# Attention with the scores of two key tiles side by side, then two value calls, two maxima tiles and two portions of filler

## The chip, the cores and the metric

The kernel runs on one core of one Trainium2 chip. The metric is device time in microseconds (us), the median of several executions; less is better. PE is TensorE (matrix multiplication), PEld its weight loads, DVE is VectorE, ACT is ScalarE, POOL is GpSimd, SP issues the DMAs. SBUF is the on-chip memory, PSUM the memory that matmuls write to.

## The reference

The whole program is one forward pass of two layers over 512 latent tokens and 256 context tokens of width 1024, all in float32: attention, a gated feed-forward network, a bidirectional Mamba-2 mixer, another feed-forward network. The change touches the attention alone, of which this is the core:

```
def gqa_attend(q, k, v):
    s = jnp.einsum('bqhgd,bkhd->bhgqk', q, k).astype(jnp.float32) * (HEAD_DIM ** -0.5)
    p = jax.nn.softmax(s, axis=-1).astype(v.dtype)
    return jnp.einsum('bhgqk,bkhd->bqhgd', p, v)
...
    # latent queries: all 512 latent and 256 context keys; context queries: the 256 context keys only
    k_all = jnp.concatenate([k_l, k_c], axis=1)
    v_all = jnp.concatenate([v_l, v_c], axis=1)
    ...
    o_c = gqa_attend(q_c, k_c, v_c).reshape(bsz, l_ctx, Q_DIM) @ w_o
```

There are 16 query heads of 64 dimensions and 4 key/value heads.

## The kernel before

Query heads are worked on in eight pairs, p = 0 to 7; a pair shares its key/value head, and its two heads lie in the two halves of the 128 partitions (`S64`). Float32 operands are split into a high and a low part (`qh`, `ql`, `kh`, `kl`), so each product is a sum of three matmuls.

`Pair.steps` runs over seven score tiles. Tiles 0 to 5 hold 128 keys each (512 latent, 256 context) against the 512 latent queries; tile 6 holds the 256 context queries against both context key tiles. For each tile PE computes the scores with keys on the partitions, in `ps_s`: three products (line 796) and a product of ones with a diagonal that subtracts each query's maximum (line 798). These matmuls contract over 64 rows, and the two heads use the two halves of the array at once (shape 64*128). ACT takes the exponential into `pr` (line 799); DVE adds the tiles into `acc` (lines 804 and 806, 810 for tile 6).

A step hands back a function for later, which the loop over pairs calls one step later: the values (`values`, line 760), probabilities times V in `ps_o`, with 64 output columns for each head side by side (shape 128*64). At tile 5 `final` follows: the sums (`ps_sum`, line 766), their reciprocal by a logarithm and an exponential on ACT (769, 770), and three DVE instructions (771 to 773: o, u, o). Tile 6 has its own values and sums in `ps_oc`, and its result goes to DRAM for pairs 0 to 5.

`Pair.maxima` is a generator with seven parts; in each, PE computes scores of the next pair with queries on the partitions (`ps_m`, line 724, shape 64*128) and DVE reduces them (line 726). The seventh part ends with the minima `mz` (742) and the diagonal `diag` (747), which the next pair's line 798 reads.

The filler is other matmuls that keep PE busy: the queries' projections of later pairs (`ps_q`), the adaptive modulation (`ps_ada`, `ps_adt`), norms (`ssq`), and the output projection of finished pairs (`ps_d`), with the ACT and DVE work that belongs to them. `Weave.step` issues about an equal share of it at each of the 56 steps, and runs "lights" (`normed` chains, weight splits) and loads that come due at numbered steps. Line numbers of the filler are 105, 106 and 108 (`mm3`), 128, 134 and 640.

The buffers that matter: `ps_s` and `ps_m` share tag S with two buffers of two PSUM banks; `ps_o`, `ps_sum`, `ps_oc` and all filler share four PSUM banks, tag B; `pr` has three buffers, `acc` one.

In this part of the program the order of each engine's instructions is set at build time by the framework's planner: it goes through program order, and takes on each engine the earliest instruction that it expects to be ready and to have its buffer. The chip then runs each engine's list in order. In the first stage of the attention (up to the query, key and value projections) the order is that of the program.

Of the kernel before, what the change touches and what calls it, by code (L numbers as in the profile page):

```python
# [7 lines left out]
P = 128  # L8
F32 = mybir.dt.float32
F32R = mybir.dt.float32r  # L10
AF = mybir.ActivationFunctionType
ALU = mybir.AluOpType
# [55 lines left out]
def t3(g, name, dt=F32, n=T):  # L68
    return g.t3p.tile([P, n], dt, tag="t3", bufs=g.n3, name=name)
# [11 lines left out]
def split(g, src, hi, lo, lo_engine="dve", pin=False):  # L81

    nc = g.nc
    keep = g.tc.keep_in_program_order if pin else lambda i: i
    keep(nc.scalar.copy(hi, src))  # L85
    eng = nc.vector if lo_engine == "dve" else nc.gpsimd
    keep(eng.tensor_tensor(lo, src, _r(hi), ALU.subtract))  # L87
# [214 lines left out]
def htiles(g, n, name):  # L302
    return tuple(g.p.tile([P, n], F32R, tag=f"h{n}", bufs=16, name=f"{p}{name}") for p in ("hh", "hl"))
# [33 lines left out]
def S(g, name):  # L337
    return g.ps.tile([P, 1024], F32, tag="S", bufs=2, name=name)


def Bank(g, name):
    return g.ps.tile([P, 512], F32, tag="B", bufs=4, name=name)
# [140 lines left out]
def attention(g, adas, project, X):  # L483


    nc, I = g.nc, g.I
    S64 = slice(0, 64), slice(64, 128)
    Bk, Sb = (lambda name: Bank(g, name)), (lambda name: S(g, name))
    t2 = lambda name, dt=F32: g.t3p.tile([P, 512], dt, tag="t2", bufs=6, name=name)
# [45 lines left out]
    acc = t3(g, "acc", n=L)  # L535
# [11 lines left out]
    e = g.p.tile([P, 2 * KT], F32, name="silu")  # L547
# [7 lines left out]
    rsl, _, _ = next(norm)  # L555
# [12 lines left out]
    for m in range(KT):  # L568
# [14 lines left out]
        if m == 4:  # L583
            rsc = t3(g, "rsc", n=C)
            pt, _, _ = next(norm)
# [26 lines left out]
    def values():  # L612
        for t in range(T // P):
            h, c0 = (hl, t * P) if t < 4 else (hc, t * P - L)
            ps = Bk("ps_v")
            for k in range(KT):
                w = tuple(w[:, (k % 4) * 256 : (k % 4 + 1) * 256] for w in wv[k // 4])
                ah, al = (a[:, c0 : c0 + P] for a in h[k])
                for i, (s, mv) in enumerate(((ah, w[0]), (ah, w[1]), (al, w[0]))):
                    nc.tensor.matmul(ps[:, :256], s, mv, start=k == 0 and i == 0, stop=k == KT - 1 and i == 2)  # L620
                yield 0.32
            nc.scalar.copy(vt[t], ps[:, :256])
# [84 lines left out]
    class Pair:  # L707
# [43 lines left out]
        def steps(self):  # L751

            (qh, ql), (kh, kl) = qprep[self.p], k2[self.kv]
            po = acc = None
            o = g.t3p.tile([P, T], F32, tag="o", bufs=2, name=f"o{self.p}")

            def values(po, pr, t, off, n, first, last):
                v = vt[t][:, self.kv * HD : (self.kv + 1) * HD]
                for e in range(2):
                    nc.tensor.matmul(po[S64[e], :n], v, pr[:, 512 * e + off : 512 * e + off + n], start=first, stop=last)  # L760

            def final(po, ps, acc, out):

                n = out.shape[-1]
                for e in range(2):
                    nc.tensor.matmul(ps[S64[e], :n], g.ones[:, :HD], acc[:, n * e : n * e + n], start=True, stop=True)
                y, u = t2("y")[:, :n], t2("u")[:, :n]

                nc.scalar.activation(y, ps, AF.Ln)
                nc.scalar.activation(y, y, AF.Exp, scale=-1.0)  # L770
                nc.vector.tensor_tensor(out, po, y, ALU.mult)
                nc.vector.scalar_tensor_tensor(u, ps, -1.0, y, ALU.mult, ALU.mult)
                nc.vector.scalar_tensor_tensor(out, u, 2.0, out, ALU.add, ALU.mult)

            def later_lat(po, pr, t, acc):
                values(po, pr, t, 0, L, t == 0, t == 5)
                if t == 5:
                    final(po, Bk("ps_sum"), acc, o[:, :L])

            def later_ctx(pr, acc):  # L780
                pc = Bk("ps_oc")
                for t in range(2):
                    values(pc, pr, 4 + t, C * t, C, t == 0, t == 1)
                final(pc[:, :C], pc[:, C:], acc, o[:, L:])
                if self.p < 6:
                    nc.sync.dma_start(odram[self.p], o)

            prev = None
            for t in range(7):
                ps, pr = Sb("ps_s"), g.t3p.tile([P, 1024], F32, tag="pr", bufs=3, name="pr")  # L790
                for q0, n, k0, off in (((0, L, t * P, 0),) if t < 6 else ((L, C, L, 0), (L, C, L + P, C))):
                    q, k = slice(q0, q0 + n), slice(k0, k0 + P)
                    outs = [ps[:, 512 * e + off : 512 * e + off + n] for e in range(2)]
                    for i, (a, b) in enumerate(((kh, qh), (kl, qh), (kh, ql))):
                        for e in range(2):
                            nc.tensor.matmul(outs[e], a[S64[e], k], b[S64[e], q], start=i == 0, stop=False)  # L796
                    for e in range(2):
                        nc.tensor.matmul(outs[e], onesr[S64[e]], self.diag[S64[e], q], start=False, stop=True)  # L798
                nc.scalar.activation(pr, ps, AF.Exp)  # L799
                if t == 0:  # L800
                    po = Bk("ps_o")
                elif t == 1:
                    acc = g.t3p.tile([P, 1024], F32, tag="acc", bufs=1, name="acc")
                    nc.vector.tensor_tensor(acc, prev, pr, ALU.add)
                elif t < 6:
                    nc.vector.tensor_tensor(acc, acc, pr, ALU.add)
                else:
                    acc = t2("accc")
                    halves = pr.rearrange("p (e k q) -> p e k q", e=2, k=2)
                    nc.vector.tensor_tensor(acc.rearrange("p (e q) -> p e q", e=2), halves[:, :, 0], halves[:, :, 1], ALU.add)  # L810
                prev = pr
                yield (lambda t=t, pr=pr, po=po, acc=acc: later_lat(po, pr, t, acc)) if t < 6 else (
                    lambda pr=pr, acc=acc: later_ctx(pr, acc))
            g.o.append(o)

    early = []
    for n, j in enumerate((0, 1, 2, 4, 5, 3)):
        ps = Bk("ps_c")
# [27 lines left out]
    def osplit(p):  # L846
        hl_, hc_ = htiles(g, L, f"ol{p}"), htiles(g, C, f"oc{p}")
        o = od.get(p, g.o[p])
        split(g, o[:, :L], *hl_)
        split(g, o[:, L:T], *hc_)  # L850
        g.oT[p] = hl_, hc_

    g.o = []
    pairs = [Pair(p) for p in range(NH // 2)]

    weave = Weave(7 * len(pairs))
# [50 lines left out]
    free = [x[0] for f in range(6) for x in (lw.get(f), lo[f]) if x]  # L907
# [5 lines left out]
    m = pairs[0].maxima()  # L913
# [8 lines left out]
        pass  # L922
    for _ in qfirst:
        pass
    late_step = None
    for p in range(NH // 2):
        m = iter(())
        if p < 7:
            for it in [it for it in weave.lights if it in {2: q2, 3: q3}.get(p + 1, qc.get(p + 1, [])) + (kk if p == 3 else [])]:
                it.run()  # L930
                weave.lights.remove(it)
            m = pairs[p + 1].maxima()
        for t, todo in enumerate(pairs[p].steps()):
            next(m, None)
            if late_step:
                late_step()
            late_step = todo
            for it in list(free):
                if it.at <= weave.now and it.ready(weave.now):
                    it.run()  # L940
                    it.when = weave.now
                    free.remove(it)
            weave.step()
            if p == 7 and t == 3:
                osplit(6)
    late_step()
    assert not weave.lights, len(weave.lights)
    weave.drain()
    osplit(7)
# [503 lines left out]
def body(nc, tc, I, out, dbg=None):  # L1453
# [36 lines left out]
    def project(fs, wo):  # L1490

        for i in range(2):
            for m in range(KT):
                down(g, [wo[f] for f in fs], [g.oT[f] for f in fs], g.mod[0][2], streams, x, [[(i, 0, streams[i][0])]], ms=[m])
                yield len(fs) * (0.69 if i == 0 else 0.36)

    attention(g, adas, project, X)
    g.tables = True
    nrm = Norm(g, 0, 4, 3, streams, "f0")
# [135 lines left out]
```

## Time and profile before

| what | us |
|---|---|
| median of 3 runs (lowest, highest) | 1904.47 (1903.81, 1907.48) |
| the profiled execution's own time | 1906.4 |
| its span, first to last instruction | 1904.2 |
| PE busy in the span | 1864.1 |
| DVE busy in the span | 1331.0 |
| ACT busy in the span | 845.4 |
| first score matmul of pair 0 | at 122.0 |
| last score matmul of pair 7 | at 385.0 |

Busy time is the time in which an engine executes an instruction; of PE it holds what a matmul's start is held up behind the one before it. In the timeline a row is the start, the duration, the engine and line, the operation with output and inputs, the array shape, the size and how many instructions were merged. Matmuls overlap, so the time that one takes of PE is the distance to the next start.

### The profile page before, as it was taken

The page shows a single profiled execution, that of the slowest core. Times are in us where ns is not written, and L with a number is a line of the kernel's source. Part 1 is how long each engine was busy: PE and PEld are TensorE (multiplying, and loading weights), DVE is VectorE, ACT ScalarE, POOL GpSimd, SP SyncE. Part 2 cuts the span into 40 slices and gives each one's busy share as a digit, 9 for nine tenths or more (in the row PEclk, how much of TensorE's full clock was granted, in tenths as well). Part 3 has the DMA queues.
Part 4 walks back from the last instruction along what each step waited for, and adds up shares of the span by engine and source line. Part 5 has one row for each costly group of instructions (what it writes and reads, how often), then busy time and mean ns, then how long its engine had stood idle before and what let it go on. Part 6 is the DMA issues. An engine that isn't in the chain of part 4 may idle for free.

```text
span 1904.2 us, 27262 instructions
## 1 busy us (share of the span) xinstructions
PE 1864.1 (98%) x10696; PEld 1528.8 (80%) x10696; DVE 1331.0 (70%) x1983; ACT 845.4 (44%) x1454; POOL 256.9 (13%) x238
## 2 busy tenths in 40 slices
PE   8899999989999999999999999999999999999999
PEld 6774545578888888888888888888888888888887
DVE  4478889678877777544478777777878576565555
ACT  3645544355122222222256767766677352323331
POOL 2300000031000000000040334443334200000000
PEclk8999999999999999999999999999999999999999
DMA  9123341014334556221222344344343323323332
GB/s 339 56 67 97 118 157 40 23 56 166 122 122 133 163 189 186 72 67 56 67 89 80 116 122 122 114 131 123 116 130 119 100 78 101 101 86 111 89 99 89
DMA packets 73424, 210.00 MB, mean 110 GB/s; under 512 B 8912, under 2 KB 14416, under 8 KB 73168
## 3 DMA queue, kind: packets, MB, share of 16 engines
q1 hardware_dynamic: 73296, 208.26, 35.1%
q8 instruction: 84, 1.38, 0.3%
q14 instruction: 44, 0.36, 0.1%
HBM read 198.79 MB, written 6.82 MB: 108 GB/s over the span
## 4 chain that ended last, share of the span: by engine, by line
PE 79%; DVE 9%; issue 3%; ACT 3%; DMA 1%; POOL 1%; SPq 0%; DVEq 0%; POOLq 0%; ACTq 0%
PE ps_up L105 10%; PE ps_up L106 10%; PE ps_up L108 10%; PE ps_d L105 6%; PE ps_d L108 6%; PE ps_d L106 6%; PE ps_in L108 4%; PE ps_in L106 4%; PE ps_in L105 4%; PE ps_o L760 2%; PE ps_s L796 2%; PE ps_st L1222 2%; DVE ht L312 1%; PE ps_wo L108 1%; PE ps_wo L105 1%
## 5 line engine op out<-in xcount | busy, mean ns | idle before, releaser
L87 DVE TENSOR_TENSOR wl<-wst,wh 128x1024 fp32r<-128x1024 f32 x209 | 260.3, 1245 | 227.7 <-PE ps_up L106 121.6
L85 ACT CAST wh<-wst 128x1024 fp32r<-128x1024 f32 x211 | 221.2, 1049 | 422.0 <-DMA wst<-in_wup 321.6
L106 PE MATMUL ps_up<-hlf,wh 128*128 128x512 f32 x1008 | 357.2, 354 | 0.0
L108 PE MATMUL ps_up<-hhf,wl 128*128 128x512 f32 x1008 | 356.9, 354 | 0.0
L105 PE MATMUL ps_up<-hhf,wh 128*128 128x512 f32 x1008 | 356.7, 354 | 0.0
L105 PEld LDWEIGHTS ps_up<-hhf,wh 128*128 128x128 f32 x1008 | 190.6, 189 | 26.5
L106 PEld LDWEIGHTS ps_up<-hlf,wh 128*128 128x128 f32 x1008 | 190.7, 189 | 26.3
L108 PEld LDWEIGHTS ps_up<-hhf,wl 128*128 128x128 f32 x1008 | 190.6, 189 | 26.4
L105 PE MATMUL ps_in<-hhs,wh 128*128 128x512 f32 (+1 forms) x560 | 204.5, 365 | 0.0
L106 PE MATMUL ps_in<-hls,wh 128*128 128x512 f32 (+1 forms) x560 | 199.5, 356 | 0.0
L108 PE MATMUL ps_in<-hhs,wl 128*128 128x512 f32 (+1 forms) x560 | 198.8, 355 | 0.0
L105 PE MATMUL ps_d<-hdh,wh 128*128 128x512 f32 (+1 forms) x568 | 193.6, 343 | 1.4 <-DVE X L970 1.2
L108 PE MATMUL ps_d<-hdh,wl 128*128 128x512 f32 (+1 forms) x568 | 193.4, 341 | 0.0
L106 PE MATMUL ps_d<-hdl,wh 128*128 128x512 f32 (+1 forms) x568 | 193.0, 340 | 0.3 <-DVE hdl L87 0.3
L970 DVE SCALAR_TENSOR_TENSOR X<-ps_d,mod,X 128x512 f32<-128x512 f32 (+1 forms) x224 | 125.0, 584 | 34.1 <-PE ps_d L108 33.8
L106 PEld LDWEIGHTS ps_d<-hdl,wh 128*128 128x128 f32 x568 | 106.7, 188 | 14.8 <-DVE hdl L87 0.7
L105 PEld LDWEIGHTS ps_d<-hdh,wh 128*128 128x128 f32 x568 | 106.3, 188 | 14.8 <-DVE X L970 1.4
L105 PEld LDWEIGHTS ps_in<-hhs,wh 128*128 128x128 f32 x560 | 106.0, 189 | 15.1 <-issue 0.9
L108 PEld LDWEIGHTS ps_in<-hhs,wl 128*128 128x128 f32 x560 | 105.9, 189 | 14.8
L108 PEld LDWEIGHTS ps_d<-hdh,wl 128*128 128x128 f32 x568 | 106.7, 188 | 13.1
L106 PEld LDWEIGHTS ps_in<-hls,wh 128*128 128x128 f32 x560 | 106.0, 189 | 13.2
L799 ACT ACTIVATE pr<-ps_s 128x1024 f32<-128x1024 f32 x56 | 57.1, 1020 | 94.0 <-PE ps_s L798 86.7
(355 smaller groups left out, 3506.4 us busy)
## 6 DMA issues: line engine op xcount, KB each, us to landing
wst<-in_wup SPq DMA_DIRECT2D x88, 512.0 KB, 3.6
wada<-in_adaT SPq DMA_DIRECT2D x56, 512.0 KB, 3.7
wst<-in_win SPq DMA_DIRECT2D x48, 512.0 KB, 3.7
wst<-in_wdown SPq DMA_DIRECT2D x44, 512.0 KB, 3.7
E<-ad SPq DMA_DIRECT2D x64, 256.0 KB, 6.7
wada<-in_adaB SPq DMA_DIRECT2D x24, 512.0 KB, 5.0
ec<-ead SPq DMA_DIRECT2D x64, 128.0 KB, 5.1
wst<-in_wout SPq DMA_DIRECT2D x16, 512.0 KB, 3.6
```

What stands on the lines that cost most here:

```text
L85: keep(nc.scalar.copy(hi, src))
L87: keep(eng.tensor_tensor(lo, src, _r(hi), ALU.subtract))
L105: mm(out, wh, ah, start=first, stop=False)
L106: mm(out, wh, al, start=False, stop=False)
L108: mm(out, wl, ah, start=False, stop=last)
L312: nc.vector.scalar_tensor_tensor(t[:, c0:c1], ap, g.moda[layer][ca][:, m, v : v + 1], rs[:, c0:c1], ALU.mult, ALU.mult)
L760: nc.tensor.matmul(po[S64[e], :n], v, pr[:, 512 * e + off : 512 * e + off + n], start=first, stop=last)
L796: nc.tensor.matmul(outs[e], a[S64[e], k], b[S64[e], q], start=i == 0, stop=False)
L799: nc.scalar.activation(pr, ps, AF.Exp)
L970: nc.vector.scalar_tensor_tensor(ap, o[:, c0:c1], gate[:, m, v : v + 1], ap, ALU.mult, ALU.add)
L1222: nc.tensor.matmul(ps[:, d * 256 : (d + 1) * 256], Bt[:, t * P : (t + 1) * P], xw[d][t], start=t == ts[0], stop=t == ts[-1])
```

## The change

`steps` now goes through the tiles in twos: 0 and 1, 2 and 3, 4 and 5, and 6 alone. It first issues the scores of both tiles (`scored`), then hands control back, then issues each tile's exponential and accumulation. The loop issues, for a double step: the scores of two tiles; the exponential of the first; the values of the first tile of the last double step; the exponential of the second; the values of the second tile of the last double step; two parts of the maxima; two steps of the filler. For tile 6 it is the same with one exponential, the two value calls of tiles 4 and 5 (with the sums), one part of the maxima and one step of filler. No instruction is added or taken away, and the buffers are as they were.

```
-            prev = None
-            for t in range(7):
-                ps, pr = Sb("ps_s"), g.t3p.tile([P, 1024], F32, tag="pr", bufs=3, name="pr")
+            def scored(t):
+                ps = Sb("ps_s")
                 for q0, n, k0, off in (((0, L, t * P, 0),) if t < 6 else ((L, C, L, 0), (L, C, L + P, C))):
...
-                nc.scalar.activation(pr, ps, AF.Exp)
-                if t == 0:
-                    po = Bk("ps_o")
...
+                return ps
+
+            prev = None
+            for t0 in range(0, 7, 2):
+                ts = range(t0, min(7, t0 + 2))
+                tiles = [scored(t) for t in ts]
+                yield None
+                for t, ps in zip(ts, tiles):
+                    pr = g.t3p.tile([P, 1024], F32, tag="pr", bufs=3, name="pr")
+                    nc.scalar.activation(pr, ps, AF.Exp)
+                    if t == 0:
+                        po = Bk("ps_o")
...
+                    prev = pr
+                    yield (lambda t=t, pr=pr, po=po, acc=acc: later_lat(po, pr, t, acc)) if t < 6 else (
+                        lambda pr=pr, acc=acc: later_ctx(pr, acc))
             g.o.append(o)
...
-    late_step = None
+    late = []
     for p in range(NH // 2):
...
-        for t, todo in enumerate(pairs[p].steps()):
-            next(m, None)
-            if late_step:
-                late_step()
-            late_step = todo
-            for it in list(free):
...
-            weave.step()
-            if p == 7 and t == 3:
-                osplit(6)
-    late_step()
+        steps = pairs[p].steps()
+        for t in range(0, 7, 2):
+            next(steps)
+            now = []
+            for i in range(min(2, 7 - t)):
+                now.append(next(steps))
+                if late:
+                    late.pop(0)()
+            for values in late:
+                values()
+            late = now
+            for _ in now:
+                next(m, None)
+            for i in range(len(now)):
+                for it in list(free):
+                    if it.at <= weave.now and it.ready(weave.now):
+                        it.run()
+                        it.when = weave.now
+                        free.remove(it)
+                weave.step()
+                if p == 7 and t + i == 3:
+                    osplit(6)
+        next(steps, None)
+    for values in late:
+        values()
```

More of the change, by code (lines that the diff above doesn't have):

```diff
@@ L798, in steps @@
                         nc.tensor.matmul(outs[e], onesr[S64[e]], self.diag[S64[e], q], start=False, stop=True)
-                nc.scalar.activation(pr, ps, AF.Exp)
-                if t == 0:
-                    po = Bk("ps_o")
[L802 to L813, printed above, removed]
+                return ps
[9 more added lines that the diff above has]
+                        po = Bk("ps_o")
+                    elif t == 1:
+                        acc = g.t3p.tile([P, 1024], F32, tag="acc", bufs=1, name="acc")
+                        nc.vector.tensor_tensor(acc, prev, pr, ALU.add)
+                    elif t < 6:
+                        nc.vector.tensor_tensor(acc, acc, pr, ALU.add)
+                    else:
+                        acc = t2("accc")
+                        halves = pr.rearrange("p (e k q) -> p e k q", e=2, k=2)
+                        nc.vector.tensor_tensor(acc.rearrange("p (e q) -> p e q", e=2), halves[:, :, 0], halves[:, :, 1],
+                                                ALU.add)
+                    prev = pr
+                    yield (lambda t=t, pr=pr, po=po, acc=acc: later_lat(po, pr, t, acc)) if t < 6 else (
+                        lambda pr=pr, acc=acc: later_ctx(pr, acc))
             g.o.append(o)
@@ L932, in attention @@
             m = pairs[p + 1].maxima()
-        for t, todo in enumerate(pairs[p].steps()):
-            next(m, None)
-            if late_step:
-                late_step()
-            late_step = todo
-            for it in list(free):
[L939 to L942, printed above, removed]
-            weave.step()
-            if p == 7 and t == 3:
-                osplit(6)
-    late_step()
+        steps = pairs[p].steps()
[23 more added lines that the diff above has]
+        values()
     assert not weave.lights, len(weave.lights)
```

## The prediction

> **What bounds the kernel now.** I read the page's first part, then the busy time of the stretch that the change touches, then the waits in it, then TensorE's (PE's) instructions one by one.
>
> ```profile
> span 1904.2 us, 27262 instructions
> PE 1864.1 (98%) x10696; PEld 1528.8 (80%) x10696; DVE 1331.0 (70%) x1983; ACT 845.4 (44%) x1454; POOL 256.9 (13%) x238
> ```
>
> PE is busy for 98% of the span, so a gain has to come from PE's own time. The profiled execution took 1906.4 us, 2.2 beyond its span, and lies 1.9 above the median of the three runs, 1904.47. My sum of differences is the same for both; I state the result against the median. The change touches only the eight pairs of heads, whose scores run from 122 to 390 us. The stretches (PE, PEld, DVE, ACT, POOL busy, then clock, DMA):
>
> ```profile
> 122.00:390.00 268.00, 261.45 (x1599) 147.55 (x1600) 220.21 (x315) 128.93 (x171) 0.00 (x0) 0.99 0.26 84
> 288.00:322.00 34.00, 32.98 (x200) 19.94 (x200) 32.93 (x51) 16.79 (x24) 0.00 (x0) 1.00 0.10 32
> ```
>
> PE is busy 261.45 of 268 us, at a granted clock of 0.99. Only 6.6 us of PE's time are idle there, so the change can hardly win from waits. VectorE (DVE) is busy 82% of the time, and 97% in one pair (288 to 322): a cover by DVE slack is thin. What looks busy, though, has loss inside it. Waits in the stretch (engine, line, releaser: total, times, longest):
>
> ```profile
> PEld ps_s L796 <- issue: 13.9, 32, 0.8
> PEld ps_o L760 <- issue: 11.4, 32, 0.4
> PE ps_s L798 <- DVE diag L747: 0.9, 2, 0.5
> ```
>
> The weight loads of the first score and the first value matmul of a step stand idle with nothing to wait for: that is where PE goes from one array shape to another. One whole step of PE shows the price (start, duration, instruction, shape, count):
>
> ```profile
> 209.14 0.40 PE L108 MATMUL ps_q<-hha,wl 128*128 128x512 f32 x1
> 209.47 0.52 PE L796 MATMUL ps_s<-qh,kh 64*128 64x512 f32 x2
> 209.81 0.41 PE L796 MATMUL ps_s<-qh,kl 64*128 64x512 f32 x2
> 210.04 0.42 PE L796 MATMUL ps_s<-ql,kh 64*128 64x512 f32 x2
> 210.28 0.42 PE L798 MATMUL ps_s<-diag,onesr 64*128 64x512 f32 x2
> 210.51 0.42 PE L724 MATMUL ps_m<-kh,qh 64*128 64x512 f32 x2
> 210.86 1.08 PE L760 MATMUL ps_o<-pr,v 128*64 128x512 f32 x4
> 211.87 0.50 PE L105 MATMUL ps_q<-hha,wh 128*128 128x512 f32 x1
> 212.20 0.40 PE L106 MATMUL ps_q<-hla,wh 128*128 128x512 f32 x1
> ...
> 213.81 0.39 PE L108 MATMUL ps_q<-hha,wl 128*128 128x512 f32 x1
> 214.13 0.50 PE L796 MATMUL ps_s<-qh,kh 64*128 64x512 f32 x2
> ```
>
> Take differences of starts. Inside one shape a slot is 0.23 (209.81 to 210.04). The last filler matmul before the scores takes 0.32 (213.81 to 214.13), the first score pair 0.34: entering costs 0.09 + 0.11 = 0.20. The maxima pair, of the scores' shape, takes 0.35: 0.12 to go over to the values. The values take 1.01 here, and 0.91 where the sums of the same shape follow (221.31 to 222.22, below): 0.10 to leave, and the first filler matmul takes 0.33, 0.10 more, so 0.20. A step of three changes of shape thus loses 0.52 of its 4.66 us.
>
> **The change part by part.** No matmul, activation, vector instruction or DMA is added or removed, and none changes size. Only PE's order, and with it what ACT and DVE have ready, moves.
>
> *Fewer changes of shape.* Two steps now: 2 x 0.52 = 1.04. A double step afterwards is scores, scores | values, values | maxima, maxima | filler, filler: in 0.20, to the values 0.12, values to maxima, maxima to filler. The last two kinds do not occur so in this order. For the values to the maxima I take the values' exit 0.10 and the scores' entry 0.11, about 0.20; for the maxima to the filler a row has both ends, where a maxima tile stands between filler matmuls:
>
> ```profile
> 274.74 0.50 PE L724 MATMUL ps_m<-kh,qh 64*128 64x256 f32 x4
> 275.18 1.06 PE L128 MATMUL ps_ada<-wada,sc 128*32 128x512 f32 x6
> ```
>
> It takes 0.44 for two slots of half width (2 x 0.12), 0.20 for entry and exit; the exit plus a filler entry of 0.10 comes to about 0.22. So a double step loses 0.20 + 0.12 + 0.20 + 0.22 = 0.74 and saves 0.30. The odd seventh tile is a step by itself with the maxima no longer beside the scores: 0.74 for 0.52, 0.22 worse. A pair saves 3 x 0.30 - 0.22 = 0.68, seven of them 4.8; the last pair has no maxima and saves 3 x 0.52 = 1.6. Together 6.4, or 44 changes fewer (21 to 16 in seven pairs, 21 to 12 in the last). In the pair of the second stretch above DVE is busy 32.93 of 34: I count that pair's 0.7 as lost, since PE would only arrive earlier at work DVE has not done. Gain 5.7; ends 4.0 (if an exit or entry is half as dear) and 6.4.
>
> The Trainium skill, TensorEngine Tiling (Array Packing), Key Properties, says that changing the tiling mode drains the engine; TensorE: Matmul & The Clock Gate, Single matmul latency, puts a drain at roughly 0.175 us. By that, an estimate, 44 changes would be worth 7.7, against 6.4 by the rows (0.145 each), and the sum below would end 1.3 lower. The trace agrees that only a change of shape pays; the rows' price stands.
>
> *The diagonal of the next pair comes later.* The seventh maxima tile feeds, on DVE, a reduction, the minima and the diagonal that the next pair's first tile needs (L798). Around a pair's end now, PE first, then DVE:
>
> ```profile
> 220.99 0.40 PE L724 MATMUL ps_m<-kh,qh 64*128 64x256 f32 x4
> 221.31 1.08 PE L760 MATMUL ps_o<-pr,v 128*64 128x512 f32 x4
> 222.22 1.03 PE L766 MATMUL ps_sum<-acc,ones 128*64 128x512 f32 x4
> 223.18 1.51 PE L640 MATMUL ssq<-qsq,ones 64*64 64x512 f32 x8
> ...
> 225.19 0.40 PE L796 MATMUL ps_s<-ql,kh 64*128 64x512 f32 x2
> 226.11 0.50 PE L798 MATMUL ps_s<-diag,onesr 64*128 64x512 f32 x2 [0.53 <-DVE diag L747]
> ```
>
> ```profile
> 221.43 1.23 DVE L726 TENSOR_REDUCE mb<-ps_m 128x4 f32<-128x1024 f32 x1 [0.66 <-PE ps_m L724]
> 222.57 0.68 DVE L810 TENSOR_TENSOR accc<-pr 128x512 f32<-128x512 f32 x1
> 223.17 0.69 DVE L742 TENSOR_TENSOR mz<-ma,mb 64x6 f32<-64x6 f32 x4
> 223.89 1.23 DVE L87 TENSOR_TENSOR wl<-wst,wh 128x1024 fp32r<-128x1024 f32 x1
> 225.03 1.02 DVE L747 TENSOR_TENSOR diag<-id,mz 128x384 fp32r<-128x384 f32 x2
> 225.97 0.69 DVE L771 TENSOR_TENSOR o<-ps_o,y 128x512 f32<-128x512 f32 x1
> 226.57 0.68 DVE L772 SCALAR_TENSOR_TENSOR u<-ps_sum,y 128x512 f32<-128x512 f32 x1
> ```
>
> From the maxima tile to L798 it takes 5.12 us and PE waits 0.53 already. Another end reads the same, 5.12:
>
> ```profile
> 320.34 0.40 PE L724 MATMUL ps_m<-kh,qh 64*128 64x256 f32 x4
> 325.46 0.50 PE L798 MATMUL ps_s<-diag,onesr 64*128 64x512 f32 x2 [0.34 <-DVE diag L747]
> ```
>
> After the change the maxima tile stands behind two value calls and the sums, so between it and L798 PE has only itself (0.35), one step's filler (nine slots, 2.1, and 0.2 of change) and three score pairs (0.80): 3.4 us. The DVE chain loses the wait for accc (0.60, done by then): 4.5. That leaves 1.1 of wait; the three diagonal-free pairs of the second score tile (3 x 0.23 = 0.69, same shape) can be put ahead of L798, 0.4 left, and I add 0.3 for ends with a short filler (ssq alone is 1.44, 223.18 to 224.62). Taken: 0.7 at seven ends, 4.9. Ends: 0 (the chain without wl and accc is 0.44 + 1.14 + 0.72 + 1.08 = 3.4, just covered) and 2.5 (with o, u and o, 3 x 0.60, put ahead of the minima).
>
> *The second probability tile waits for a buffer.* There are three pr buffers. Of tiles 2a and 2a+1, the second exponential needs the buffer that the first value call of the same double step frees, and the second maxima tile needs the score bank (two, S) that this exponential frees. How ACT follows PE:
>
> ```profile
> 183.00 0.40 PE L798 MATMUL ps_s<-diag,onesr 64*128 64x512 f32 x2
> 183.43 1.02 ACT L799 ACTIVATE pr<-ps_s 128x1024 f32<-128x1024 f32 x1 [4.02 <-PE ps_s L798]
> ...
> 211.70 1.69 ACT L669 CAST kl<-kl 64x768 fp32r<-64x768 f32 x2
> 213.29 1.01 ACT L799 ACTIVATE pr<-ps_s 128x1024 f32<-128x1024 f32 x1
> ```
>
> ACT starts 0.20 after PE's slot is over (0.43 after its start) and needs 1.02: the bank is free 1.22 after the first value call. PE gets there after the second call and its exit (1.01) and the first maxima pair (0.34): 1.35. It fits by 0.1 if ACT is free. It isn't always: the scores of 210.28 got their exponential at 213.29, 2.6 late, behind casts. ACT is busy with other work for (128.93 - 56 x 1.02)/268 = 27%, in pieces of about 0.9: a mean delay of 0.12 on 21 double steps with maxima, 2.5 us. Ends: 0, and 8 (0.4 each).
>
> *Filler in twos* moves no DMA to another queue; its loads are issued from the same step numbers. Two reductions now come together on DVE (2 x 1.14, perhaps an accumulation of 1.14 ahead, 0.44 to start: 3.9) while PE has maxima and two fillers, about 5.1, until it wants the bank back: hidden, 1.2 to spare, and past that each us of DVE backlog is a us of PE wait. Before, a single reduction had a whole step.
>
> Sum: -5.7 + 4.9 + 2.5 = +1.7. Against the profiled execution 1908.1, against the median 1906.2.
>
> **The rivals.** *The gain goes through*: the framework's planner, which orders each engine's instructions at build time by program order among what it expects to be ready, covers the pair's end with other matmuls and ACT keeps up. Speaking for it: now only 0.9 us of PE wait at L798 in total. Then -6.4 and about 1.2 of rests: 1899.3.
>
> *The pair's end turns into a wait* (slower): the lat result's o, u, o (three DVE instructions, 0.60 apart) are earlier in the program than the minima and come ahead of them when their input is ready as the reduction ends. Then 1.8 a pair: -5.7 + 7 x 1.8 + 2.5 = +9.4, 1913.9. It decides the sign from a wait of about 0.5 a pair (-5.7 + 2.5 + 7w = 0), and is measurably slower from 1.0. For it: DVE at 82%, and both ends shown wait already. Against: now the planner puts them behind the diagonal (225.97).
>
> *The groups do not hold*: where the planner finds the second maxima bank not free, it puts that tile among filler matmuls, as at 274.74, for two more changes (0.20 + 0.22). In all 21: 8.8 in place of 2.5, +8.0, 1912.5. For it: margin 0.1 only. Against: the order mostly follows the program now.
>
> **How the numbers follow.** Gain and waits about cancel: 0.37, forecast 1906.2, its own range 1901 to 1909. Gain goes through: 0.25. Wait at the pair's end: 0.27. Groups split: 0.11. Plus or minus 0.2% is 3.8 us, about what the runs (1903.81 to 1907.48) can tell from no change. Faster 0.25; same 0.37; slower 0.38. Range from the first rival, 1898.5, to just beyond the slower ones, 1915.
>
> **What would show it.** Right: waits of score and value weight loads for "issue" fall to about half in times; a maxima tile after the values starts about 0.1 late; the wait of L798 for the diagonal grows from 0.9 to about 5 us; waits of ps_m for the exponential appear, 2 to 3 us. Wrong: diagonal waits near 0 (faster) or above 10 (slower); maxima tiles among the filler; the stretch from the first scores to the last shorter than 262 or longer than 276 us; or a difference outside it.

## The result: slower by about 9 us, and the profile after

The changed kernel took 1915.24 us (median of 6 runs, 1911.37 to 1918.11), the one before beside it 1907.38 (6 runs, 1903.81 to 1908.53). The ratio is 1.0048, 95% interval 1.0034 to 1.0063: 9 us slower (6.5 to 12). Below, "us against before" is always (ratio - 1) x 1904 from runs of both kernels on the same chip.

The page after, first lines, then three stretches: before the first score, up to the last, behind it. In a stretch's line stand its length, the busy time and number of instructions of PE, PEld, DVE, ACT and POOL, then the granted clock, the busy share of the DMA engines and GB/s.

```profile
span 1915.2 us, 27247 instructions
PE 1870.3 (98%) x10696; PEld 1533.3 (80%) x10696; DVE 1330.0 (69%) x1983; ACT 845.2 (44%) x1454; POOL 255.6 (13%) x238
...
0.00:121.00 121.00, 108.23 (x704) 86.30 (x704) 67.27 (x127) 59.01 (x105) 24.59 (x23) 0.92 0.48 168
121.00:394.00 273.00, 262.32 (x1563) 148.65 (x1562) 218.37 (x311) 126.64 (x168) 0.00 (x0) 1.00 0.25 82
394.00:1915.00 1521.00, 1499.76 (x8436) 1298.36 (x8432) 1044.40 (x1545) 659.59 (x1181) 230.97 (x215) 1.00 0.36 110
```

The same stretches before:

```profile
0.00:122.00 122.00, 108.86 (x702) 87.03 (x702) 67.16 (x127) 59.01 (x105) 24.43 (x23) 0.92 0.48 167
122.00:385.00 263.00, 256.45 (x1567) 144.34 (x1566) 217.95 (x311) 126.68 (x168) 0.00 (x0) 0.99 0.26 85
385.00:1904.00 1519.00, 1498.77 (x8434) 1297.39 (x8430) 1045.92 (x1545) 659.67 (x1181) 232.46 (x215) 1.00 0.36 110
```

Ten of the 11 us between these two executions lie in the middle stretch: 273 us instead of 263. PE is busy for 6 us more there with the same matmuls, and idle for 11 us instead of 6.5. A matmul's busy time also holds what its start is held up, so a part of the 6 us can be waiting too; how much is not shown. The waits of the stretch, PE's own and then its weight loads':

```profile
PE ps_s L797 <- DVE diag L747: 6.1, 5, 1.9
PE ps_ada L128 <- DMA wada<-in_adaB: 2.2, 3, 1.7
...
PEld ps_o L760 <- issue: 19.5, 62, 0.8
PEld ps_m L724 <- issue: 9.3, 12, 0.8
PEld ps_s L797 <- DVE diag L747: 8.3, 5, 2.4
PEld ps_m L724 <- ACT pr L807: 8.2, 17, 0.8
PEld ps_s L795 <- issue: 6.6, 13, 0.8
```

The wait for the diagonal is 6.1 us (0.9 before; the line is 797 now). The scores' waits with nothing to wait for fell from 13.9 us in 32 times to 6.6 in 13 as promised, but those of the values rose from 11.4 in 32 to 19.5 in 62, and those of the maxima, which had none of note, are 9.3. In the list of PE's instructions between the first and the last score there are 172 changes of array shape; before there were 178. I had counted on 44 fewer, and there are 6 fewer.

Where they went is seen at a pair's end. PE, then DVE:

```profile
185.93 1.03 PE L766 MATMUL ps_sum<-acc,ones 128*64 128x512 f32 x4
186.88 0.50 PE L724 MATMUL ps_m<-kh,qh 64*128 64x256 f32 x4
187.32 1.92 PE L128 MATMUL ps_ada<-wada,sc 128*32 128x512 f32 x16
189.17 0.50 PE L795 MATMUL ps_s<-qh,kh 64*128 64x512 f32 x2
...
190.46 0.39 PE L795 MATMUL ps_s<-ql,kh 64*128 64x512 f32 x2
190.77 1.08 PE L760 MATMUL ps_oc<-pr,v 128*64 128x256 f32 x6
193.00 0.74 PE L797 MATMUL ps_s<-diag,onesr 64*128 64x512 f32 x4 [1.15 <-DVE diag L747]
193.66 0.43 PE L760 MATMUL ps_oc<-pr,v 128*64 128x256 f32 x1
...
194.67 1.07 PE L640 MATMUL ssq<-qsq,ones 64*64 64x512 f32 x2
195.67 0.74 PE L724 MATMUL ps_m<-kh,qh 64*128 64x256 f32 x6
```

```profile
187.43 1.22 DVE L726 TENSOR_REDUCE mb<-ps_m 128x4 f32<-128x1024 f32 x1 [1.24 <-PE ps_m L724]
188.57 0.68 DVE L771 TENSOR_TENSOR o<-ps_o,y 128x512 f32<-128x512 f32 x1
189.17 0.68 DVE L772 SCALAR_TENSOR_TENSOR u<-ps_sum,y 128x512 f32<-128x512 f32 x1
189.77 0.32 DVE L742 TENSOR_TENSOR mz<-ma,mb 64x6 f32<-64x6 f32 x2
190.10 0.69 DVE L773 SCALAR_TENSOR_TENSOR o<-u,o 128x512 f32<-128x512 f32 x1
190.81 0.35 DVE L742 TENSOR_TENSOR mz<-ma,mb 64x6 f32<-64x6 f32 x2
191.19 0.69 DVE L130 COPY ada_sb<-ps_ada 128x512 f32<-128x512 f32 x1
191.91 1.03 DVE L747 TENSOR_TENSOR diag<-id,mz 128x384 fp32r<-128x384 f32 x2
```

On DVE o, u and o stand among and ahead of the minima and the diagonal is done at 192.9. At five of the seven ends all three stand ahead of the diagonal, at one o alone, and at one o and u between its two halves; in the kernel before they stand behind it at all seven. On PE the planner has moved up what it had: the second tile's three score pairs, then part of the context values. The diagonal's product comes back between the values: scores, values, scores, values in place of scores, values. PE waits 1.15 us all the same, and the maxima behind stand in the filler. On PE the same five ends look like this one; one has the context values whole, one is split further.

### The profile page after: what moved, and what is told of

Read it like the earlier page. It is cut to its first block, busy times and chain, and to the rows that moved or that the text cites. A ratio compares the mean times of both kernels' runs of the same rounds, so it can differ in the third digit from the quotient of the medians.

```text
span 1915.2 us, 27247 instructions
## 1 busy us (share of the span) xinstructions
PE 1870.3 (98%) x10696; PEld 1533.3 (80%) x10696; DVE 1330.0 (69%) x1983; ACT 845.2 (44%) x1454; POOL 255.6 (13%) x238
## 4 chain that ended last, share of the span: by engine, by line
PE 78%; DVE 10%; issue 3%; ACT 2%; POOL 1%; DMA 1%; SPq 0%; DVEq 0%; POOLq 0%; ACTq 0%
PE ps_up L105 10%; PE ps_up L106 10%; PE ps_up L108 10%; PE ps_d L105 6%; PE ps_d L108 6%; PE ps_d L106 6%; PE ps_in L108 4%; PE ps_in L106 4%; PE ps_in L105 4%; PE ps_o L760 2%; PE ps_st L1242 2%; PE ps_s L795 1%; PE ps_wo L108 1%; PE ps_wo L105 1%; PE ps_wo L106 1%
## 5 line engine op out<-in xcount | busy, mean ns | idle before, releaser
L106 PE MATMUL ps_d<-hdl,wh 128*128 128x512 f32 (+1 forms) x568 | 192.9, 340 | 0.3 <-DVE hdl L87 0.3
L167 DVE SCALAR_TENSOR_TENSOR junk<-wada,cb 128x1024 f32<-128x1024 f32 x80 | 97.5, 1218 | 1.2 <-ACT cb L158 0.8
```

Of the source, the lines that this page charges most:

```text
L106: mm(out, wh, al, start=False, stop=False)
L167: g.tc.keep_in_program_order(nc.vector.scalar_tensor_tensor(junk, w, 1.0, cb[:, v * D : (v + 1) * D], ALU.mult, ALU.mult, accum_out=md[:, ...
```

## The experiments

**Theory A**: the diagonal is late at the pair's end, by waiting and by what is put in front of it. **B**: in the middle of a pair the second maxima tile hangs on the second exponential and its bank. **C**: the splitting of the groups is the loss, whatever causes it.

*The diagonal earlier* (`e1_early_diag`):

```
-            for _ in now:
+            for _ in range((2, 2, 3, 0)[t // 2]):
                 next(m, None)
```

> The changed kernel with the parts of the maxima issued 2, 2, 3, 0 in the four groups of a pair instead of 2, 2, 2, 1: the last part, which makes the next pair's diagonal, comes one double step earlier; nothing else moves. Planned changes of array shape between the first and the last score: 160 (172 in the changed kernel, 178 in the one before). Theory A (the late diagonal at the pair's end makes the loss, by waiting at L797 and by the values that the planner puts in front of it): the 6.1 us of diagonal waits fall under 1 and the time comes down by 6 to 10 us, to between -1 and +3 us of the kernel before. Theory B (the loss is in the middle of a pair, where the second maxima tile waits for the second exponential's bank): three maxima tiles in a group make it no better; +8 us or more against before.

Measured: ratio 1.0013 (1.0002 to 1.0024), +2.5 us against before. The wait for the diagonal is gone from the list.

*The pair's end as before, double steps as changed* (`e2_odd_first`):

```
             now = []
+            if t == 6:
+                next(m, None)
...
-            for _ in now:
+            for _ in now if t < 6 else ():
```

> The changed kernel, but in the group of the seventh tile the last part of the maxima goes ahead of the two value calls, where it stood before the change; the double steps are as changed. Planned changes of shape 142. Theory A: the diagonal is in time again, its waits fall from 6.1 to about 1 us, the values are no longer split around it, and 30 changes of shape fewer save 3 to 5 us more: 1 to 4 us below the kernel before. Theory B: only the pair's end is mended, the waits of the second maxima tile for the exponential (8.2 us of weight-load waits) stay: +4 to +7 us against before.

Measured: 0.9993 (0.9983 to 1.0002), -1.3 us, no measurable difference from before and 10 us better than the change. Changes of shape: 142. Both runs say A, against B alone. They do not tell A from C, since the changes fell with the wait, from 172 to 160 and 142.

*The pair's end alone, on the kernel before* (`e13_end_only`): the last maxima part moves behind the values of tile 5 and the sums, once a pair.

```
-            next(m, None)
+            if t < 6:
+                next(m, None)
             if late_step:
                 late_step()
+            if t == 6:
+                next(m, None)
```

> The kernel before with one part of the change alone: at the seventh tile only, the last maxima part goes behind the value call of tile 5 and the sums. Seven instructions groups in the whole program move. Planned changes of shape 202 (before 178), because the planner fills the wait for the diagonal with maxima, values and filler. If the late diagonal is the cause: 24 changes at 0.14 to 0.2 (3 to 5 us) and 2 to 5 us of waits, +5 to +10 against before, about what the whole change lost. If it isn't: within 3 us of before.

Measured: 1.0034 (1.0021 to 1.0048), +6.5 us. Seven groups moved a microsecond or two later cost two thirds of what the whole change lost. Waits of this kernel's stretch, PE, then weight loads:

```profile
PE ps_s L798 <- DVE diag L747: 2.2, 3, 1.1
...
PEld ps_s L798 <- DVE diag L747: 4.5, 5, 1.5
```

Only 2.2 us are PE's open waits (0.9 before), and PE's idle time in the stretch is that of the kernel before (6.7 and 6.5 us). Its busy time is 5.6 us longer, at 24 more changes of shape with which the planner fills the wait. At 0.2 each they would make 4.8; that they are the larger part fits, but is argued.

*Every step's maxima behind its values, on the kernel before* (`e4_max_late`), the two calls exchanged:

> The kernel before with one part of the change alone: in each single step the maxima part goes behind the values instead of ahead of them. Planned changes of shape 230 instead of 178. If a change of shape costs what the rows say (0.2 for each further group of scores or maxima): 52 x 0.14 to 0.2 = 7 to 10 us, and theory A adds the late diagonal at seven ends, 3 to 7 us: +10 to +17 against before. If only the changes of shape count: +7 to +10, with diagonal waits as before, about 1 us.

Measured: 1.0032 (1.0019 to 1.0044), +6 us, as e13 within the intervals: below both expectations. That does not make the 28 more changes than in e13 free. In the profiles the stretch from the first score to the last is 274.8 us in e4 and 268.8 in e13; the whole times agree because e4's first score comes at 115.3 us and e13's at 120.1, for which no cause is shown. Of these 6.0 us up to 3.4 can be the clock: in e4 the granted clock is one half for 6.8 us of the stretch, in e13 never. That leaves, as an estimate from these figures, 0.1 to 0.2 us for each further change.

*No filling: PE pinned to program order in the pair loop*, once with the change (`e5_pe_order`), once with the pair's end mended (`e6_odd_pe`), once in the kernel before (`e9_before_pe`):

```
+    man = g.tc.manual_schedule(engines={ET.PE})
+    man.__enter__()
     late = []
     for p in range(NH // 2):
...
+    man.__exit__(None, None, None)
```

> The changed kernel with TensorE's instructions of the pair loop pinned to program order, so that the planner can put nothing between the groups; the other engines' order is still planned. Planned changes of shape 125 instead of 172. Theory C (the planner's splitting of the groups is the loss, the waits are small): about 47 x 0.14 = 6.6 us less than the changed kernel, +2 to +3 against before. Theory A: the diagonal now comes 1 to 2.5 us late at each of seven pair ends with nothing to fill, 7 to 17 us of waits at L797; +6 to +14 against before.

> The kernel of e2 (the seventh tile's last maxima part ahead of the values) with TensorE's instructions of the pair loop pinned to program order. Planned changes of shape 118 (e2: 142). Pinned without this repair the time was +29 us. If the late diagonal made that (16.2 us of waits at L797 in that run), they go to under 2 us here and the time falls by 14 us or more, to +4 to +14 against before. If pinning is dear by itself, because single transfers and other engines' results come later than the planner thinks, whatever the diagonal does, it stays above +18.

> Control for pinning: the kernel before, nothing else changed, with TensorE's instructions of the pair loop pinned to program order. Planned changes of shape 165 (before: 178). If pinning alone is cheap here: within 5 us of before, so the +29 of the pinned changed kernel is its order. If pinning is dear by itself: +10 to +25.

Measured: 1.0152 (1.0138 to 1.0166), 1.0064 (1.0050 to 1.0077), 1.0039 (1.0027 to 1.0051): +29, +12 and +7 us. With 125 changes of shape instead of 172 the changed kernel is far slower still. Waits of e5:

```profile
PE ps_s L797 <- DVE diag L747: 16.2, 7, 3.8
PE ps_adt L134 <- DVE qsq L653: 3.4, 1, 3.4
PE ps_s L795 <- DVE ma L726: 3.1, 3, 1.5
```

Unfilled, the diagonal is 2.3 us late at each of seven ends. But pinning changes the clock too, which the expectations left out. The stretch from the first score to the last in e5, e6 and e9:

```profile
118.40:410.80 292.40, 260.36 (x1561) 154.58 (x1562) 219.30 (x311) 127.66 (x168) 0.00 (x0) 0.95 0.23 76
119.40:393.60 274.20, 252.72 (x1562) 151.14 (x1562) 217.71 (x311) 126.65 (x168) 0.00 (x0) 0.97 0.25 82
117.80:388.30 270.50, 258.40 (x1567) 148.22 (x1566) 218.37 (x311) 126.98 (x168) 0.00 (x0) 0.97 0.25 83
```

The granted clock is 0.95, 0.97 and 0.97, against 1.00 in the changed kernel: it is one half for 31, 17 and 17 us. A score matmul that takes 0.39 us elsewhere takes up to 0.79 there, so this can cost up to half of these times, an estimate: 15, 8.5 and 8.5 us. Even without 15 of its 29 us e5 is slower than the changed kernel, with fewer changes of shape, so C falls as the only cause. Mending the end takes 17 us off (29 - 12); PE's idle time in the stretch falls by 10.5 (32.0 to 21.5), since other waits grow where the diagonal's 16.2 go, and up to 7 are the clock. So whether waiting is dearer than the planner's filling, where mending the end takes off 10 us, is not shown. Pinning itself costs 7 us in the kernel before, in waits (12.1 us idle, 6.5 without) and clock.

**What eats the gain of the double steps?** e2 has 36 changes fewer than before and wins 1.3 us, 3 at most. In its stretch PE is busy for 252.8 us instead of 256.5, but idle for 12.0 instead of 6.5: the shapes win about 4, and waits take it. Its second maxima tile at a pair's start; PE, then ACT:

```profile
188.35 0.60 PE L766 MATMUL ps_oc<-accc,ones 128*64 128x256 f32 x4
188.89 0.50 PE L724 MATMUL ps_m<-kh,qh 64*128 64x256 f32 x4
191.55 0.52 PE L724 MATMUL ps_m<-kh,qh 64*128 64x512 f32 x2 [2.16 <-ACT pr L807]
...
186.63 1.03 ACT L807 ACTIVATE pr<-ps_s 128x1024 f32<-128x1024 f32 x1 [1.72 <-PE ps_s L797]
189.53 1.04 ACT L85 CAST wh<-wst 128x1024 fp32r<-128x1024 f32 x1 [1.87 <-DMA wst<-in_wq]
190.48 1.02 ACT L807 ACTIVATE pr<-ps_s 128x1024 f32<-128x1024 f32 x1
```

ACT stood 1.87 us before a cast whose transfer had not landed; the exponential that frees the bank stood behind it.

*Filler ahead of the maxima in a pair's first group* (`e7_g0_fill`, on e2):

```
-            for _ in now if t < 6 else ():
+            for _ in now if 0 < t < 6 else ():
                 next(m, None)
...
                 weave.step()
+                if t + i == 0:
+                    for _ in now:
+                        next(m, None)
```

> The kernel of e2 with one step of the filler ahead of the two maxima parts in a pair's first group, where only the last context values stand between the scores and the maxima and where e2's profile shows TensorE waiting for the second exponential (5.7 us in 7 waits). Planned changes of shape 148 (e2: 142). If these waits are what is left of the loss: -5.7 + 6 x 0.2 = -4.5 against e2, 4 to 6 us below before. If ACT's delay is only passed on to the next group: same as e2 within 1.5 us.

Measured: 1.0000 (0.9992 to 1.0009), the same as e2 within the intervals. Weight-load waits, e2 first, then e7:

```profile
PEld ps_m L724 <- ACT pr L807: 11.5, 18, 2.4
PEld ps_s L795 <- DVE ma L726: 1.1, 3, 0.4
```

```profile
PEld ps_s L795 <- DVE ma L726: 7.3, 10, 1.8
PEld ps_m L724 <- ACT pr L807: 6.2, 12, 1.0
```

The wait is passed on: the maxima, later now, free their banks later, and the next scores wait for the reduction.

*Four probability buffers* (`e8_odd_pr4`, on e2): `bufs=4` for pr, 16 in place of 18 row buffers.

> The kernel of e2 with four probability buffers instead of three (the room comes from two of the 18 row buffers), so that the second exponential of a double step no longer needs the first value call to be over. Planned changes of shape 138 (e2: 142). If the buffer is what delays the second maxima tile: the weight-load waits of ps_m for the exponential (11.5 us in e2) halve, 2 to 4 us below e2. If ACT's other work is what delays the exponential, as in the first group, where no value call holds a buffer: within 1.5 us of e2, the waits stay at 8 us or more; fewer row buffers could cost up to 3 us.

Measured: 1.0053 (1.0041 to 1.0065), +10 us. Inconclusive for the buffer: with fewer row buffers the first score came at 126.8 us (117.6 in e2), and the loss lies ahead of the pairs; from the first score to the last the two profiles have 262.2 and 264.8 us. The maxima's weight loads wait 17.7 us for the exponential, not less.

*Without most of the maxima* (`e15_before_few`, `e16_odd_few`): the step orders of the kernel before and of e2, with five of seven maxima parts replaced by copies, and the queries scaled down by 1000 so that nothing overflows. These kernels leave out the true maxima. One of the copies:

```
-                scores((t,), 0, L, lat)
+                nc.vector.tensor_copy(lat[:, :, t : t + 1], lat[:, :, 4:5])
```

> A control that leaves work out: the kernel before with five of the seven maxima parts of each pair replaced by small copies (the first and the last stay, and so does the diagonal's place), and the queries scaled down by 1000 so that nothing overflows. Its time alone says little: 5 fewer score tiles and reductions in seven pairs, 35 x 0.23 = 8 us less for PE and 43 us less for DVE; 7 to 12 us below before.

> The kernel of e2 with the same work left out as in e15. Planned changes of shape 117 (e15: 170): 13 fewer groups of scores or maxima and 16 fewer of filler at 0.2, 24 fewer of values at 0.07: 7.5 us. If the maxima's share of the two score banks took the double steps' gain: 6 to 9 us below e15. If the gain is lost elsewhere (ACT's exponentials, the pr buffers): 0 to 3 us below e15.

Measured: 0.9898 (0.9881 to 0.9915) and 0.9854 (0.9834 to 0.9873). e15 lost more work than I reckoned (-19 us). The double steps win 8.4 us here (0.0044 x 1904; the intervals do not overlap), about the 7.5 of the shapes; with all maxima they won 1.3. So their gain is there, and what comes with the maxima takes it. Whether that is their part in the two score banks or their load on DVE, which is busy for 181 us of the stretch here and for 217 in e2, these runs do not tell apart.

*Double steps where there are no maxima* (`e11_pair7`): `by = 2 if p == 7 else 1`.

> The double steps of the change only in the last pair, which has no maxima; pairs 0 to 6 as in the kernel before. Planned changes of shape 169 (before 178). The rows gave 1.6 us for this pair, and nothing waits there: 1.0 to 2.0 us below before. If double steps win nothing even without maxima: within 0.5.

Measured: 0.9994 (0.9985 to 1.0003), -1.1 us; the size expected, but not told from zero.

*Only the filler in twos*, on the kernel before (`e10_fill2`), and with pair 7 doubled (`e12_fill_pair7`): `for i in range((0, 2, 0, 2, 0, 2, 1)[t])` around the filler's step.

> The kernel before with one part of the change alone: the filler of two steps stands together after every second step (none after tiles 0, 2, 4; two steps' worth after 1, 3, 5; one after 6). Scores, maxima and values keep their places in each single step, so the diagonal is as early as before. Planned changes of shape 165 (before 178; 22 fewer groups of filler-shaped matmuls, some more among the others). If a group of filler costs 0.2 and the banks' waits stay covered by a step's scores and values: 3 to 5 us below before. If two score tiles without filler between them wait for their banks: within 2 us of before, and the waits of the scores for the maxima's reduction show it.

> Both together: the filler in twos of e10 in pairs 0 to 6, the double steps in pair 7. Planned changes of shape 159. The sum of the two: 4 to 6 us below before if e10 wins, 1 to 3 if it does not. The candidate to beat both kernels.

Measured: 1.0005 (0.9993 to 1.0017) and 0.9997 (0.9985 to 1.0008), no difference. In e10 the second score tile now waits for the first one's exponential:

```profile
PEld ps_s L796 <- ACT pr L799: 10.7, 14, 1.1
```

*Weight casts two steps later* (`e14_split_late` on e2, `e17_before_split` on the kernel before, `e18_after_split` on the change):

```
-        return first, Light(spl, at, lambda now: first.when is not None and now >= first.when + 2)
+        return first, Light(spl, at, lambda now: first.when is not None and now >= first.when + 4)
...
-    wsplit = lambda p: Light(lambda: wq_split(p), 0, lambda now: jobs[p].began is not None and now >= jobs[p].began + 2)
+    wsplit = lambda p: Light(lambda: wq_split(p), 0, lambda now: jobs[p].began is not None and now >= jobs[p].began + 4)
```

The first of these lines also serves the splits of the finished heads' outputs (`osplit`), which therefore come later too.

> The kernel of e2 with the weight casts of the query and output projections two steps later after their loads (four steps instead of two), so that ACT does not stand before a cast whose transfer has not landed while the second exponential waits behind it. If such casts are what held the second exponential: the waits of the maxima for it (5.7 us in e2) fall to 3 or less, 2 to 4 us below e2. If the two-bank chain of scores and maxima limits anyway: within 1.5 us of e2, with another wait in their place.

> Control for e14: the kernel before with nothing but the weight casts two steps later after their loads. Planned changes of shape 175 (before 178). If the casts hurt only the double steps, in which the second maxima tile hangs on the second exponential: within 3 us of before, and e14's 7 us are the double steps' gain let through. If the later casts are a gain by themselves: 5 to 8 us below before, as e14.

> The changed kernel itself with the weight casts two steps later; the diagonal is late as changed. Planned changes of shape 174 (changed 172). With the late diagonal worth about 10 us whatever the casts do: +1 to +5 us against before, the casts returning 4 to 8 of its 9. If the casts were the main cause and the diagonal hardly matters: 3 us or more below before.

Measured: 0.9963 (0.9950 to 0.9975), 0.9966 (0.9956 to 0.9976) and 1.0023 (1.0012 to 1.0034): -7, -6.5 and +4.4 us. e14, at 1896.58 us, beats both kernels, and the wait of its maxima for the exponential is 1.4 us instead of 5.7. But the control wins as much without the change: the later casts are a gain by themselves, and double steps with the diagonal in time add nothing to it that the whole times can tell. (From the first score to the last the two profiles have 254.7 us in e14 and 259.4 in e17, one execution each.) My reading that the casts hold up the double steps alone falls. The 11 us between e18 and e14 are again the pair's end. Which wait the later casts take away in the kernel before is not shown.

## Why the prediction was wrong

I forecast no change (1906.2, from 1898.5 to 1915.0); measured was 1915.24 and a ratio clear of 1. The step that failed is the pair's end. The gain and the second exponential together were forecast at -5.7 + 2.5 = -3.2 us, and e2 against the kernel before measured -1.3. The pair's end was forecast at +4.9, and the change against e2, which differ only in the place of the last maxima part, measured +10.5. By the steps:

- *A change of shape costs 0.2 for each further group of scores or filler*: about right. In the changed kernel two value calls take 1.86 us for eight slots of 0.228, so 0.04 over, and the maxima behind them 0.78 for slots of 0.47, 0.31 over:

```profile
202.16 1.94 PE L760 MATMUL ps_o<-pr,v 128*64 128x512 f32 x8
204.02 0.84 PE L724 MATMUL ps_m<-kh,qh 64*128 64x512 f32 x6
204.80 1.05 PE L134 MATMUL ps_adt<-cst,ada_sb 128*128 128x2 f32 x8
```

  I had reckoned 0.42 for these two, and they lose 0.35. e16 against e15 shows the gain itself, 8.4 us, where most maxima are out of the way. The Trainium skill, TensorEngine Tiling (Array Packing), Key Properties, says that a change of the tiling mode drains the engine. These rows agree in that the loss sits at the changes; at 0.04 and 0.31 us they have no single price.
- *44 changes fewer*: wrong for the order that runs. I counted them in the program's order, and there it is about so: the pinned kernels have 165 and 125. The planner made 172 of it, 6 fewer than before. My rival "the groups do not hold" named this for the second maxima tile; but 30 of the 38 that are missing came back at the pair's end (e2 has 142), where I had taken it for granted that filling costs no change.
- *The diagonal's delay, 0.7 at each of seven ends, 4.9*: too small. Mending the end returns 10 us, and doing it alone costs 6.5, so 0.9 to 1.5 an end, waits and further changes together; the open waits alone are 6.1 us. I had reckoned a chain without o, u, o on DVE, and at five of seven ends all three go ahead of the diagonal. Without filling the wait is 2.3 an end, near the upper end that I had put (2.5, with o, u, o first). The row of the kernel before in which DVE did the diagonal first did not speak for the kernel after: there the sums' reciprocal was ready after the reduction had ended (224.6 and 222.7 us), here before it (188.3 and 188.7). I had this as a rival, with 0.27, and its time of 1913.9 was the nearest. Its mechanism is the one that the runs show; that its time fits so well is partly luck, since it had 2 us too much for the ends (12.6 against 10.5) and 2 us too much gain from the rest (-3.2 against -1.3), and the two cancel.
- *The second exponential, 2.5*: too small, and the cover for *filler in twos* (1.2 us to spare at the banks) did not hold as told. What is measured is the two together: with the maxima about 7 of the 8.4 us go (e16 against e15, beside e2's 1.3). Which of exponential, reduction and buffer it is changes from group to group (e7, e10); the buffer alone stays open, since e8 lost its time elsewhere.
- *No DMA or later stage is touched*: right; behind the last score the profiles have 1521 and 1519 us.
- *The signs*: "issue" waits of the values' weight loads rose where I had them halve, so their count does not follow the changes of shape. The band of 262 to 276 us for the stretch came from a window of 268 that ends 5 us behind the last score; by the same measure as the 273 us now it was 263 before, so 273 inside the band does not speak for the forecast.

## What to carry to other kernels

Before grouping work by its shape on TensorE, list what the moved groups were feeding: a group whose result comes back to the same engine through another one's chain should keep its place, unless the wait has been shown to be cheaper than what the shapes win. Here one maxima tile a pair, moved behind two value calls and the sums, turned no measurable change (-1.3 us) into a loss of 9 us. Count changes of shape in the order that is built, not in the program, and when the gain is lost to buffers in turn, removing one wait only shows the next.

## What the runs showed of the hardware that was not expected

The kernels with PE pinned to program order were granted half the clock for 17 to 31 us of the stretch between the first and the last score, where PE idles for 12 to 32 us; the kernels that the planner ordered, for 0 to 7 us. So pinning does not show the price of waits alone, and whether a low clock came from the waits is not shown. And ACT, in order, stood 1.87 us before a cast whose 512 KB had not landed, with the exponential behind it; four steps instead of two between such a load and its cast are worth 6.5 us in the kernel before, with the steps of its pairs as they were (175 changes of shape instead of 178).
